# Activation, product and operand parts of an expert made for 64 or 128 slots by a branch on ScalarE and VectorE

## The chip, the cores and the metric

The kernel runs on one core of a Trainium2 chip. It uses TensorE for matrix products, VectorE and ScalarE for elementwise work, GpSimd a little, and SyncE for starting DMA transfers. Each engine works through an instruction queue of its own, and semaphores order them against each other. In the rows PE is TensorE (PEld its loading of the stationary operand), DVE is VectorE, ACT is ScalarE and SP is SyncE; a q behind a name means the engine's instruction queue. The metric is the device time of one execution in microseconds.

## The reference

A trunk of two layers on 256 tokens of width 1024, all in float32. Each layer has a mixer (gated linear attention and an SSD group) and a feed-forward part. The first layer's feed-forward part is dense, the second's is a mixture of 8 experts of which each token uses 2, and that is where the change is:

```python
def swiglu(t, w_gate, w_up, w_down):
    return (jax.nn.silu(t @ w_gate) * (t @ w_up)) @ w_down

top_v, top_i = lax.top_k(logits, TOP_K)
top_p = jax.nn.softmax(top_v, axis=-1)
gates = jnp.sum(jax.nn.one_hot(top_i, N_EXPERTS) * top_p[..., None], axis=1)
for e in range(N_EXPERTS):
    out = out + gates[:, e:e + 1] * swiglu(t, w_gate[e], w_up[e], w_down[e])
```

`w_gate[e]` and `w_up[e]` are 1024 x 3584, `w_down[e]` is 3584 x 1024.

## The kernel before

For each expert the kernel gathers the expert's tokens into slots (128 of them; a second pass behind the loop serves experts with more than 128 tokens, and is skipped here). The products are made from operands split in two parts, a rounded one and the rest, so that a product is a sum of three terms.

**Weights.** Every weight item is 1 MB in float32. SyncE's queue issues its transfer (`pump`, L154) into one of a few raw buffers as soon as one is free. ScalarE copies the item, rounded, into a slot (L182), VectorE subtracts the copy from the raw item into a second slot (L183), and from then on the raw buffer is free for the next transfer.

**An expert's loop.** `run_experts` walks through the items in the order of `moe_order`. The 3584 columns of an expert form 7 chunks of 512. A chunk has six items, G0 G1 (gate), U0 U1 (up) and D0 D1 (down) of the chunk before it. Behind certain items the dictionary `due` places the elementwise work: `copied` (ScalarE, L1229) brings a product out of PSUM; `gate` folds or transposes it on TensorE and applies Silu on ScalarE (L1253); `hidden` does the same for the up product and multiplies on VectorE (L1257); `parted` makes the two operand parts of the result, a copy on ScalarE (L1262) and a subtraction on VectorE (L1263). The tile `fsg` holds activation and product, `fth` the operand parts that the down product (`y`) uses.

**Narrow and wide.** `few[e]` is 1 where an expert has at most 64 tokens. `is_narrow` (L1578) loads it into a register of TensorE, and `modal` (L1177) makes a branch on it. In the narrow body of `mm_slots` the two operand parts of 64 slots lie side by side in one matmul's 128 columns (L1187), so that an item needs two matmuls per block and not three (L1189, L1190, and L1193 in both). The narrow body of `folded` adds the two halves of such a product with a matmul (L1238); the wide body transposes (L1240). Before the change only TensorE branches. ScalarE and VectorE do the same work for all 128 slots in either case.

**The next expert.** `at` hangs the next expert's preparation on items of this one: at chunk 3 the register and a slot map, at chunk 4 the gathering (TensorE) and splitting (`split_cols`: four ScalarE operations, a VectorE cast and a VectorE subtraction) of two halves of its operand, and between these two halves `slots_T`, for which VectorE makes a small tile `pm` (`pairs`, L1483) that TensorE transposes (L1508) and VectorE rounds off (L1511).

Of the kernel before, what the change touches and what calls it, by code (L numbers as in the profile page):

```python
# [50 lines left out]
def trunk(ctx: ExitStack, tc: tile.TileContext, a: dict, out: bass.AP):  # L51
# [1168 lines left out]
    def run_experts(mo, experts, operand, fold, at):  # L1220
# [11 lines left out]
        def folded(src, narrow, p):  # L1232

            def body(nar):
                for k in range(4):
                    ks = slice(k * P, (k + 1) * P)
                    if nar:
                        pe.matmul(p[:, ks], src[:, ks], fold, start=True, stop=True)  # L1238
                    else:
                        pe.transpose(p[:, ks], src[:, ks], ident)  # L1240

            modal(narrow, body)
            return p
# [7 lines left out]
        def gate(key):  # L1251
            sil[key] = mo.tile([P, FC], F, name=nm("fsg"), tag="fsg")
            act.activation(sil[key], folded(gs.pop(key), ops[key[0]][1], ps_t()), AF.Silu)  # L1253

        def hidden(key):
            p, s = folded(us.pop(key), ops[key[0]][1], ps_mm()), sil[key]
            dve.tensor_tensor(s, p, s, op=OP.mult)  # L1257

        def parted(key):
            t = th[key] = mo.tile([P, 4, P, 2], R, name=nm("fth"), tag="fth", bufs=2)  # L1260
            sv = sil.pop(key).rearrange("p (k t) -> p k t", k=4)
            act.activation(t[:, :, :, 0], sv, AF.Copy)  # L1262
            dve.tensor_tensor(t[:, :, :, 1], sv, t[:, :, :, 0].bitcast(F), op=OP.subtract)  # L1263

        for n, (kind, e, c, i) in enumerate(order):
# [3 lines left out]
            X, narrow = ops[e]  # L1269
# [71 lines left out]
    def moe(mo, ys, row, mT):  # L1341
# [235 lines left out]
        def is_narrow(e):  # L1577
            return pe.value_load(few[0:1, e:e + 1], min_val=0, max_val=1)  # L1578

        narrow = {0: is_narrow(0)}  # L1580
        pT = {0: slots_T(0, pm, narrow=narrow[0])}
        m = {"pm": pm, "y": {}, "acc": None}

        def free():
            return ps_y(1 - turn[0])

        def at(e, c, t, ys):
# [20 lines left out]
            if e < NE - 1:  # L1608
# [3 lines left out]
                if where == (4, 1):  # L1612
                    split_cols(*gathered(e + 1, 0), *gather(m["pm"], 0, free))
                if where == (4, 3):
                    pT[e + 1] = slots_T(e + 1, m["pm"], free, narrow[e + 1])
                if where == (4, 5):
                    split_cols(*gathered(e + 1, 1), *gather(m["pm"], 1, free))
# [12 lines left out]
        y = run_experts(mo, list(range(NE)), lambda e: (xg[e % 2], narrow[e]), fold, at)  # L1630
# [12 lines left out]
        with tc.If(over > 0):  # L1643
            xg.clear()
            for e in range(NE):
# [9 lines left out]
                y = run_experts(mo, [e], lambda e: (xg[e % 2], None), fold, lambda *_: None)  # L1655
# [129 lines left out]
```

## Time and the profile before

| | us |
|---|---|
| median of three runs | 1551.8 (1550.6 to 1554.3) |
| the profiled execution's own time | 1550.5 |
| its span | 1548.7 |
| TensorE busy in the span | 1410.1 (91%) |
| VectorE busy | 1310.8 (85%) |
| ScalarE busy | 1068.9 (69%) |
| expert phase in the span | 575 to 1531.6 |

The span is cut at the profile's first and last instruction. A busy share over the whole span mixes the first layer, the mixer and the expert phase, which have different limits. For the change only the expert phase matters, and inside it the experts with at most 64 tokens and those with more have to be looked at apart. The granted TensorE clock of the run is 0.967 of full speed.

### The profile page before, as it was taken

To read this page: it belongs to the slowest core of one execution; us is meant where nothing else is said; L and a number is where in the kernel's file an instruction comes from. 1 tells how busy PE (TensorE), PEld (TensorE's weight loads), DVE (VectorE), ACT (ScalarE), POOL (GpSimd) and SP (SyncE) were. 2 spreads that over 40 slices of the span, in tenths; PEclk is the share of its full clock that TensorE was granted. 3 is DMA by queue.
4 is the path that set the end of the run, shared out by engine and by line. 5 is a ranking of instruction groups with operands and counts; after the bars stand their busy time and mean duration, and the time that the engine had idled before them with its cause. 6 is when DMAs were issued, how large, how long until landed. Compare 5 with 4: busy or idle time off the path is not lost.

```text
span 1548.7 us, 20698 instructions
## 1 busy us (share of the span) xinstructions
PE 1410.1 (91%) x7578; PEld 1203.0 (78%) x7578; DVE 1310.8 (85%) x1171; ACT 1068.9 (69%) x1259; POOL 41.0 (3%) x68
## 2 busy tenths in 40 slices
PE   4998899999999877999999988989899999999986
PEld 3877699999888765878878767767778888878864
DVE  7898877777766758999879989989999888878996
ACT  3475554455557447987768779879898777768875
POOL 2001000000010100000000000000000000000001
PEclk8999999999999988999999989999999999999988
DMA  9975688888834454999979999999999999979992
GB/s 331 304 248 175 246 296 311 309 291 304 293 137 136 165 190 168 392 376 397 353 275 371 392 336 399 397 367 397 398 399 395 394 335 350 347 269 373 384 372 106
DMA packets 204603, 483.15 MB, mean 312 GB/s; under 512 B 13119, under 2 KB 15405, under 8 KB 204462
## 3 DMA queue, kind: packets, MB, share of 16 engines
q1 hardware_dynamic: 203890, 480.05, 85.1%
q8 instruction: 98, 1.61, 0.4%
q10 hardware_dynamic: 428, 0.63, 0.1%
q0 software_dynamic: 144, 0.52, 0.1%
q14 instruction: 43, 0.35, 0.1%
HBM read 480.12 MB, written 1.05 MB: 311 GB/s over the span
## 4 chain that ended last, share of the span: by engine, by line
PE 69%; DVE 15%; ACT 7%; issue 6%; DMA 2%; POOL 1%; DVEq 0%; ACTq 0%; SPq 0%; POOLq 0%
PE mm L1193 9%; DVE ws L183 6%; PE y L1193 6%; PE mm L1189 5%; PE mm L1190 5%; PE mm L1187 5%; PE mm L409 4%; PE mm L410 4%; PE mm L408 4%; PE y L1187 4%; PE y L408 3%; PE y L410 3%; PE y L409 3%; ACT ws L182 3%; PE y L1189 3%
## 5 line engine op out<-in xcount | busy, mean ns | idle before, releaser
L183 DVE TENSOR_TENSOR ws<-raw,ws 128x2048 fp32r<-128x2048 f32 x280 | 633.6, 2285 | 68.6 <-ACT ws L182 67.3
L182 ACT ACTIVATE ws<-raw 128x2048 fp32r<-128x2048 f32 x280 | 530.3, 1917 | 108.4 <-PE y L1190 34.4
L174 ACT ACTIVATE ws<-raw 128x1024 fp32r<-128x1024 f32 x138 | 145.9, 1061 | 133.7 <-PE mm L410 63.5
L175 DVE TENSOR_TENSOR ws<-raw,ws 128x1024 fp32r<-128x1024 f32 x138 | 166.7, 1220 | 56.0 <-ACT ws L174 55.6
L1193 PE MATMUL y<-ws,fth 128*128 128x512 f32 x448 | 128.4, 410 | 0.0
L1193 PE MATMUL mm<-ws,hTh 128*128 128x512 f32 x448 | 122.0, 394 | 1.1 <-DVE ws L183 1.1
L1193 PE MATMUL mm<-ws,hTl 128*128 128x512 f32 x448 | 121.8, 394 | 0.0
L347 DVE SCALAR_TENSOR_TENSOR ada<-raw,s_col,ada 128x1024 f32<-128x1024 f32 (+1 forms) x98 | 115.6, 1180 | 2.1
L183 DVE TENSOR_TENSOR ws<-xm,ws 128x2048 fp32r<-128x2048 f32 x46 | 105.2, 2287 | 9.3 <-ACT ws L182 8.9
L408 PE MATMUL mm<-hTh,ws 128*128 128x256 f32 x384 | 107.9, 281 | 0.0
L1193 PEld LDWEIGHTS y<-ws,fth 128*128 128x128 f32 x448 | 90.7, 202 | 20.7
L409 PE MATMUL mm<-hTh,ws 128*128 128x256 f32 x384 | 106.8, 278 | 0.0
L410 PE MATMUL mm<-hTl,ws 128*128 128x256 f32 x384 | 106.7, 278 | 0.0
L1193 PEld LDWEIGHTS mm<-ws,hTh 128*128 128x128 f32 x448 | 85.5, 191 | 20.2 <-DVE ws L183 1.6
L1193 PEld LDWEIGHTS mm<-ws,hTl 128*128 128x128 f32 x448 | 85.7, 191 | 18.1
L182 ACT ACTIVATE ws<-xm 128x2048 fp32r<-128x2048 f32 x46 | 88.3, 1920 | 12.2 <-PE mm L1190 6.6
L1187 PE MATMUL mm<-ws,hTh 128*128 128x512 f32 x336 | 94.9, 405 | 0.5 <-ACT ws L182 0.5
L1187 PE MATMUL y<-ws,fth 128*128 128x512 f32 x280 | 87.4, 438 | 6.8 <-DVE fth L1263 6.8
L1189 PE MATMUL mm<-ws,hTl 128*128 128x512 f32 x224 | 89.9, 401 | 0.0
L1190 PE MATMUL mm<-ws,hTl 128*128 128x512 f32 x224 | 88.5, 395 | 0.0
L1262 ACT ACTIVATE fth<-fsg 128x512 fp32r<-128x512 f32 x56 | 37.7, 673 | 64.6 <-DVE fsg L1257 64.5
L409 PEld LDWEIGHTS mm<-hTh,ws 128*128 128x128 f32 x384 | 72.3, 188 | 0.2
(381 smaller groups left out, 2816.4 us busy)
## 6 DMA issues: line engine op xcount, KB each, us to landing
raw<-in_moe_w_down SPq DMA_DIRECT2D x95, 1024.0 KB, 8.3
raw<-in_moe_w_up SPq DMA_DIRECT2D x94, 1024.0 KB, 8.1
raw<-in_moe_w_gate SPq DMA_DIRECT2D x92, 1024.0 KB, 7.3
raw<-in_ada_w SPq DMA_DIRECT2D x48, 1024.0 KB, 6.0
raw<-in_w_in SPq DMA_DIRECT2D x21, 1024.0 KB, 5.3
xm<-in_moe_w_up SPq DMA_DIRECT2D x16, 1024.0 KB, 5.9
xm<-in_moe_w_down SPq DMA_DIRECT2D x15, 1024.0 KB, 7.2
xm<-in_moe_w_gate SPq DMA_DIRECT2D x15, 1024.0 KB, 8.6
```

What stands on the lines that cost most here:

```text
L174: act.activation(h, src, AF.Copy)
L175: dve.tensor_tensor(lo, src, h.bitcast(F), op=OP.subtract)
L182: act.activation(h, r, AF.Copy)
L183: dve.tensor_tensor(lo, r, h.bitcast(F), op=OP.subtract)
L347: dve.scalar_tensor_tensor(acc, w, s_col[:, k:k + 1], acc, op0=OP.mult, op1=OP.add)
L408: pe.matmul(ps, xh, wh, start=start, stop=False)
L409: pe.matmul(ps, xl, wh, start=False, stop=False)
L410: pe.matmul(ps, xh, wl, start=False, stop=stop)
L1187: pe.matmul(ps, xs[:, 0:HALF].rearrange("p s two -> p (s two)"), wh, start=start, stop=False)
L1189: pe.matmul(ps, xs[:, :, 0], wh, start=start, stop=False)
L1190: pe.matmul(ps, xs[:, :, 1], wh, start=False, stop=False)
L1193: pe.matmul(ps, both if nar else xs[:, :, 0], wl, start=False, stop=stop)
```

## The change

`folded` loses its own branch. `gate`, `hidden` and `parted` each put their whole body into one branch: the folds on TensorE together with ScalarE's Silu; the folds with VectorE's product; ScalarE's copy with VectorE's subtraction. `blocks` cuts the tiles to the first 64 of each 128 columns in the narrow body, so a 128x512 operation becomes 128x4x64. `split_slots` does the same around `split_cols` for the next expert. `is_narrow` loads a second register, on TensorE, ScalarE and VectorE; TensorE's `mm_slots` and `slots_T` keep the first one.

```diff
--- before.py
+++ after.py
@@ -1229,18 +1229,18 @@
             act.activation(out, p, AF.Copy)
             return out
 
-        def folded(src, narrow, p):
-
-            def body(nar):
-                for k in range(4):
-                    ks = slice(k * P, (k + 1) * P)
-                    if nar:
-                        pe.matmul(p[:, ks], src[:, ks], fold, start=True, stop=True)
-                    else:
-                        pe.transpose(p[:, ks], src[:, ks], ident)
-
-            modal(narrow, body)
+        def folded(src, nar, p):
+
+            for k in range(4):
+                ks = slice(k * P, (k + 1) * P)
+                if nar:
+                    pe.matmul(p[:, ks], src[:, ks], fold, start=True, stop=True)
+                else:
+                    pe.transpose(p[:, ks], src[:, ks], ident)
             return p
+
+        def blocks(t, nar):
+            return t.rearrange("p (k t) -> p k t", k=4)[:, :, :HALF if nar else P]
 
         def put(n, f, *args):
             due.setdefault(n, []).append((f, args))
@@ -1249,24 +1249,41 @@
             (gs if kind == "G" else us)[key] = copied("gs" if kind == "G" else "us", ps.pop((kind,) + key))
 
         def gate(key):
-            sil[key] = mo.tile([P, FC], F, name=nm("fsg"), tag="fsg")
-            act.activation(sil[key], folded(gs.pop(key), ops[key[0]][1], ps_t()), AF.Silu)
+            src, p = gs.pop(key), ps_t()
+            s = sil[key] = mo.tile([P, FC], F, name=nm("fsg"), tag="fsg")
+
+            def body(nar):
+                folded(src, nar, p)
+                act.activation(blocks(s, nar), blocks(p, nar), AF.Silu)
+
+            modal(ops[key[0]][2], body)
 
         def hidden(key):
-            p, s = folded(us.pop(key), ops[key[0]][1], ps_mm()), sil[key]
-            dve.tensor_tensor(s, p, s, op=OP.mult)
+            src, p, s = us.pop(key), ps_mm(), sil[key]
+
+            def body(nar):
+                folded(src, nar, p)
+                sv = blocks(s, nar)
+                dve.tensor_tensor(sv, blocks(p, nar), sv, op=OP.mult)
+
+            modal(ops[key[0]][2], body)
 
         def parted(key):
             t = th[key] = mo.tile([P, 4, P, 2], R, name=nm("fth"), tag="fth", bufs=2)
-            sv = sil.pop(key).rearrange("p (k t) -> p k t", k=4)
-            act.activation(t[:, :, :, 0], sv, AF.Copy)
-            dve.tensor_tensor(t[:, :, :, 1], sv, t[:, :, :, 0].bitcast(F), op=OP.subtract)
+            s = sil.pop(key)
+
+            def body(nar):
+                sv, tv = blocks(s, nar), t[:, :, :HALF if nar else P]
+                act.activation(tv[:, :, :, 0], sv, AF.Copy)
+                dve.tensor_tensor(tv[:, :, :, 1], sv, tv[:, :, :, 0].bitcast(F), op=OP.subtract)
+
+            modal(ops[key[0]][2], body)
 
         for n, (kind, e, c, i) in enumerate(order):
             key = (e, c)
             if (kind, c, i) == ("G", 0, 0):
                 ops[e] = operand(e)
-            X, narrow = ops[e]
+            X, narrow, _ = ops[e]
             if kind in "GU" and not i:
                 ps[(kind,) + key] = ps_mm()
             if (kind, c, i) == ("D", 0, 0):
@@ -1575,14 +1592,25 @@
         fill()
 
         def is_narrow(e):
-            return pe.value_load(few[0:1, e:e + 1], min_val=0, max_val=1)
+            f = few[0:1, e:e + 1]
+            return pe.value_load(f, min_val=0, max_val=1), nc.values_load(
+                f, engines=[mybir.EngineType.PE, mybir.EngineType.Activation, mybir.EngineType.DVE], min_val=0, max_val=1)
 
         narrow = {0: is_narrow(0)}
-        pT = {0: slots_T(0, pm, narrow=narrow[0])}
+        pT = {0: slots_T(0, pm, narrow=narrow[0][0])}
         m = {"pm": pm, "y": {}, "acc": None}
 
         def free():
             return ps_y(1 - turn[0])
+
+        def split_slots(e, hf):
+            dst, (src, scale, shift) = gathered(e, hf), gather(m["pm"], hf, free)
+
+            def body(nar):
+                w = HALF if nar else P
+                split_cols(*[d[:, :, :w] for d in dst], src[:, :, :w], scale, shift)
+
+            modal(narrow[e][1], body)
 
         def at(e, c, t, ys):
             nonlocal acc, fnw
@@ -1610,11 +1638,11 @@
                     narrow[e + 1] = is_narrow(e + 1)
                     m["pm"] = slot_map(e + 1, 0)
                 if where == (4, 1):
-                    split_cols(*gathered(e + 1, 0), *gather(m["pm"], 0, free))
+                    split_slots(e + 1, 0)
                 if where == (4, 3):
-                    pT[e + 1] = slots_T(e + 1, m["pm"], free, narrow[e + 1])
+                    pT[e + 1] = slots_T(e + 1, m["pm"], free, narrow[e + 1][0])
                 if where == (4, 5):
-                    split_cols(*gathered(e + 1, 1), *gather(m["pm"], 1, free))
+                    split_slots(e + 1, 1)
             elif where in ((2, 5), (3, 3)):
                 t = c - 2
                 for hf in range(2):
@@ -1627,7 +1655,7 @@
                 m["y"][0] = y_split(ys[e], 0, g2)
 
         acc = fnw = None
-        y = run_experts(mo, list(range(NE)), lambda e: (xg[e % 2], narrow[e]), fold, at)
+        y = run_experts(mo, list(range(NE)), lambda e: (xg[e % 2],) + narrow[e], fold, at)
         extra.remove("xm")
         sq, write = finisher(fnw)
         y1 = mo.tile([P, 512], F, name=nm("ys"), tag="us")
@@ -1652,7 +1680,7 @@
                 assert state["next"] == first_item
                 pump()
                 fill()
-                y = run_experts(mo, [e], lambda e: (xg[e % 2], None), fold, lambda *_: None)
+                y = run_experts(mo, [e], lambda e: (xg[e % 2], None, None), fold, lambda *_: None)
                 for hf in range(2):
                     combine(e, pT, y_split(y, hf, g2), hf, False, acc)
             sq, write = finisher(load_fnw())
```

On VectorE, one chunk of expert 0 (`fsg` the activation and product, `fth` the operand parts, `ws` and `raw` weight slots and raw buffers). Before:

```order
L183 TENSOR_TENSOR ws_6328<-raw_794_6046,ws_6327 128x2048
L1257 TENSOR_TENSOR fsg_6267<-mm_6333,fsg_6267 128x512
L1177 UNCONDITIONAL_BRANCH
L183 TENSOR_TENSOR ws_6367<-raw_801_6096,ws_6366 128x2048
L1263 TENSOR_TENSOR fth_6372<-fsg_6267,fth_6372 128x512
L183 TENSOR_TENSOR ws_6397<-raw_804_6123,ws_6396 128x2048
```

After:

```order
L183 TENSOR_TENSOR ws_6394<-raw_795_6098,ws_6393 128x2048
L1177 COMPARE_AND_BRANCH
L1267 TENSOR_TENSOR fsg_6333<-mm_6399,fsg_6333 128x4x64
L1177 UNCONDITIONAL_BRANCH
L1267 TENSOR_TENSOR fsg_6333<-mm_6399,fsg_6333 128x512
L1177 UNCONDITIONAL_BRANCH x2
L183 TENSOR_TENSOR ws_6434<-raw_802_6149,ws_6433 128x2048
L1177 COMPARE_AND_BRANCH
L1278 TENSOR_TENSOR fth_6439<-fsg_6333,fth_6439 128x4x64
L1177 UNCONDITIONAL_BRANCH
L1278 TENSOR_TENSOR fth_6439<-fsg_6333,fth_6439 128x512
L1177 UNCONDITIONAL_BRANCH x4
```

The subtractions L183 stand where they stood. The product (L1257, now L1267) and the subtraction of the operand parts (L1263, now L1278) each stand twice, behind a compare: in four blocks of 64 and in 512 columns. An UNCONDITIONAL_BRANCH is a jump over the other body or to the next block.

On ScalarE, the same chunk, from the copy of the up product. Before:

```order
L1229 ACTIVATE us_6265<-mm_6212 128x512
L1253 ACTIVATE fsg_6267<-pt_6268 128x512
L1177 UNCONDITIONAL_BRANCH x2
L182 ACTIVATE ws_6300<-raw_791_6019 128x2048
L182 ACTIVATE ws_6327<-raw_794_6046 128x2048
L1177 UNCONDITIONAL_BRANCH x2
```

After:

```order
L1229 ACTIVATE us_6330<-mm_6277 128x512
L1177 COMPARE_AND_BRANCH
L1257 ACTIVATE fsg_6333<-pt_6332 128x4x64
L1177 UNCONDITIONAL_BRANCH
L1257 ACTIVATE fsg_6333<-pt_6332 128x512
L1177 UNCONDITIONAL_BRANCH x2
L182 ACTIVATE ws_6366<-raw_792_6071 128x2048
L1177 UNCONDITIONAL_BRANCH
L182 ACTIVATE ws_6393<-raw_795_6098 128x2048
L1177 COMPARE_AND_BRANCH
L1177 UNCONDITIONAL_BRANCH x3
```

The Silu (L1253, now L1257) stands twice behind a compare, and in front of the next subtraction's copy there is a second compare, that of the up product's branch, in which ScalarE has no work. The order of the working instructions is unchanged on each engine. In the whole program ScalarE and VectorE have 183 compares each where they had 1, TensorE 527 where it had 457, and the registers are loaded 9 times on ScalarE and VectorE (1 before) and 17 times on TensorE (9 before).

## Rows read from the trace of the kernel before

**Rows 1.** The page's part 1: busy us (share of the span) xinstructions, one line.
```profile
PE 1410.1 (91%) x7578; PEld 1203.0 (78%) x7578; DVE 1310.8 (85%) x1171; ACT 1068.9 (69%) x1259; POOL 41.0 (3%) x68
```

**Rows 2.** Experts 0 to 7 by stretch, expert 0 from 612: window, length, engines, PEclk, DMA share, GB/s.
```profile
575.00:689.30 114.30, 98.74 (x468) 80.66 (x467) 102.47 (x75) 95.08 (x80) 0.00 (x0) 0.91 0.83 304
689.30:822.40 133.10, 129.68 (x597) 108.32 (x596) 112.34 (x72) 98.58 (x81) 0.00 (x0) 0.99 0.95 347
822.40:935.40 113.00, 101.52 (x502) 84.33 (x500) 106.12 (x71) 93.06 (x80) 0.00 (x0) 0.95 0.99 368
935.40:1049.40 114.00, 100.39 (x492) 82.84 (x492) 108.72 (x72) 94.67 (x81) 0.00 (x0) 0.96 1.02 387
1049.40:1158.00 108.60, 98.62 (x493) 81.49 (x492) 108.38 (x72) 94.43 (x81) 0.00 (x0) 0.98 1.04 398
1158.00:1285.60 127.60, 127.60 (x598) 107.23 (x596) 113.75 (x73) 100.20 (x82) 0.00 (x0) 1.00 1.01 375
1285.60:1420.70 135.10, 131.68 (x605) 109.98 (x603) 111.56 (x72) 98.59 (x81) 0.76 (x1) 0.99 0.92 327
1420.70:1531.60 110.90, 101.39 (x475) 83.07 (x474) 107.37 (x71) 88.33 (x71) 0.00 (x0) 0.95 0.89 334
612.00:689.30 77.30, 73.21 (x371) 60.68 (x369) 76.53 (x50) 68.69 (x60) 0.00 (x0) 0.98 1.01 374
```

**Rows 3.** The page's part 5, TensorE's narrow matmul into y: busy, mean ns, idle before.
```profile
L1187 PE MATMUL y<-ws,fth 128*128 128x512 f32 x280 | 87.4, 438 | 6.8 <-DVE fth L1263 6.8
```

**Rows 4.** Waits of VectorE, ScalarE and SyncE's DMA queue, 822.4 to 1158: total us, times, longest.
```profile
DVE ws L183 <- ACT ws L182: 10.9, 7, 3.6
ACT fth L1262 <- DVE fsg L1257: 36.7, 19, 3.5
SPq L154 <- DVE ws L183: 268.3, 119, 6.9
```

**Rows 5.** Groups by page or tile (min/median/max ns, first to last start): VectorE, ScalarE durations.
```profile
L183 DVE TENSOR_TENSOR ws<-raw,ws 128x2048 fp32r<-128x2048 f32 x280 | 633.6, 2285 | 68.6 <-ACT ws L182 67.3
L1511 DVE TENSOR_SCALAR pTs<-y x7: 415/424/425, 658.3 to 1375.8; 128x256 fp32r<-128x256 f32 x7
L1257 DVE TENSOR_TENSOR fsg<-mm,fsg x56: 674/682/686, 604.6 to 1527.4; 128x512 f32<-128x512 f32 x56
L1253 ACT ACTIVATE fsg<-pt x56: 582/596/635, 595.4 to 1525.4; 128x512 f32<-128x512 f32 x56
L1262 ACT ACTIVATE fth<-fsg x56: 653/676/692, 605.3 to 1528.1; 128x512 fp32r<-128x512 f32 x56
```

**Rows 6.** Branches and register loads by line: count, min/median/max ns, first to last start.
```profile
L1177 PEldq COMPARE_BRANCH  x741: 63/176/396, 564.0 to 1530.0; - x186
L1643 DVEq COMPARE_BRANCH  x1: 72/72/72, 1539.7 to 1539.7; - x1
L1643 DVEq EVENT_SEMAPHORE  x1: 21/21/21, 1542.6 to 1542.6; - x1
L1643 PEldq COMPARE_BRANCH  x1: 3665/3665/3665, 1535.6 to 1535.6; - x1
L1642 DVEq TENSOR_LOAD <-cmi x1: 545/545/545, 1539.1 to 1539.1; - x1
```

**Rows 7.** VectorE's timeline in a chunk of expert 4: start us, us, instruction.
```profile
1102.45 2.28 DVE L183 TENSOR_TENSOR ws<-raw,ws 128x2048 fp32r<-128x2048 f32 x1
1104.65 0.68 DVE L1263 TENSOR_TENSOR fth<-fsg,fth 128x512 fp32r<-128x512 f32 x1
```

**Rows 8.** TensorE's wait for pm (total, longest; then by timeline), and two stretches around such places.
```profile
PE y L1508 <- DVE pm L1483: 13.6, 2, 6.8
899.25 0.73 PE L1508 MATMUL y<-ident,pm 128*128 128x128 f32 x2 [6.82 <-DVE pm L1483]
900.00:920.00 20.00, 20.00 (x93) 16.79 (x94) 14.38 (x11) 14.82 (x15) 0.00 (x0) 0.87 0.82 290
1015.00:1035.00 20.00, 20.00 (x100) 16.89 (x100) 15.28 (x11) 15.78 (x15) 0.00 (x0) 0.93 0.96 350
```

## The prediction

> **What bounds the kernel now.** I read the page's engine line first, then a table that cuts the expert phase into one stretch per expert, then the waits of the narrow stretch 822.4 to 1158, then single rows. Over the whole span TensorE leads with 1410.1 us, VectorE follows with 1310.8 and ScalarE has 1068.9 [rows 1], but this is an average over stages with different limits. The page's row of the narrow matmul into `y` has x280, that is 5 experts times 7 chunks times 8 [rows 3]: five of the eight experts have at most 64 tokens. The stretches say which. In experts 1, 5 and 6 TensorE is busy for 129.68 of 133.10, 127.60 of 127.60 and 131.68 of 135.10 us, and moves more instructions (597 to 605): these are the wide ones, and TensorE sets their time. Experts 0, 2, 3, 4 and 7 have only 468 to 502 matmuls and some 100 us of TensorE in 108 to 114, with VectorE above it: 106.12, 108.72, 108.38 and 107.37 in experts 2, 3, 4 and 7, and in expert 0, once its start is over, 76.53 of 77.30 [rows 2]. So in the narrow experts VectorE is the engine without a gap.
>
> It is not alone there. In expert 4 the DMA engines move 398 GB/s at a share of 1.04, and no stretch of this table shows more; experts 2 and 3 have 368 and 387. Experts 0 (from 612 us) and 7 have 374 and 334, so there the transfers have a reserve [rows 2]. The two are tied together: the queue that issues the weight transfers waits 119 times for a VectorE subtraction (L183), 268.3 us in all, since a raw buffer is free only when VectorE has read it. VectorE itself waits little for ScalarE, 10.9 us in 335, while ScalarE waits 36.7 us for the product L1257, so ScalarE has room [rows 4].
>
> **The change, part by part.** *VectorE's narrow product and operand part* (L1257, L1263): each of the 35 narrow chunks runs them on 256 elements per partition where it ran 512. No row of exactly this form exists, so I take the slope of VectorE's own rows: 2285 ns for 2048 elements and 682 for 512 give 1603/1536 = 1.04 ns per element, 0.267 us for 256 elements. A check is the 128x256 row of L1511: 424 ns, where 682 less 267 is 415 [rows 5]. Two such instructions give 0.53 us per chunk. From below, the saving is bounded at nothing if four blocks of 64 with gaps cost as much as 512 straight elements; from above at the whole 0.68 each. I take the slope, because the 424 ns row is so near.
>
> *ScalarE's narrow Silu and copy* (L1253, L1262): 596 and 676 ns at 512 elements [rows 5]. The cover is that ScalarE is busy for 94.43 of 108.60 us [rows 2] and waits for VectorE, not the other way round. At VectorE's slope it would save some 0.27 us each; I count nothing on the path. If ScalarE became the late one, this saving would help too.
>
> *The two operand halves of the next expert* shrink in the same way, 512 to 256 elements in a cast and a subtraction, 0.53 us on VectorE per half. Four experts gain it, but those of experts 2 and 7 are made inside wide experts, where TensorE hides it. The other two add 1.1 us each to VectorE's lead inside experts 2 and 3; I count it as reserve, since what I count there is limited otherwise (below).
>
> *TensorE's folds* keep their instructions and order. It passes 70 more branches (the operand parts and halves, which hold nothing for it). In the trace 741 such branches took 63 to 396 ns, median 176 [rows 6], and the queue reaches them while earlier matmuls run. I count nothing. If that cover were gone in the wide experts, 27 extra branches (21 chunks and 6 halves) at 0.176 would be 4.8 us.
>
> *Branches on ScalarE and VectorE* are new. Each chunk brings three to either engine (gate, product and part; one of the three is empty for each), each a compare and, on the narrow side, a jump over the other half. Nothing in the trace shows such branches on these engines inside the loop. The nearest rows are TensorE's, 176 ns for a compare and 63 for a jump, and VectorE's own compare after the loop, 72 ns [rows 6]. What hides them: VectorE's instructions of a narrow chunk stand back to back. L183 starts at 1102.45 and takes 2.28, L1263 starts at 1104.65 [rows 7], so its queue dispatches ahead of the one that is running. A branch behind a 2.28 us subtraction has that long to be decided. Behind the branches stand the next subtractions, and for these wait TensorE and the transfer queue. Bounds: nothing at one end, 3 x (0.176 + 0.063) = 0.72 us per chunk at the other. I take nothing, because two of the three branches stand behind a full subtraction; both ends are in the range.
>
> [...]
>
> *The second register* is loaded once per expert, on TensorE, ScalarE and VectorE. VectorE's load after the loop took 545 ns [rows 6]. At the head of the phase nothing is queued that could hide it, and I let one of the other seven be seen: 2 x 0.545 = **+1.1 us**.
>
> *Where the gain goes.* Expert 0 from 612 us: VectorE has no gap and the transfers a reserve, five chunks x 0.53 = **-2.7**. Expert 7: seven x 0.53 = **-3.7**. Wide experts: 0. Experts 2 to 4 form one run, and at 398 GB/s the transfers are full. What they can still gain is the time in which they slacken. At 899 us TensorE waits 6.8 us for VectorE's small `pm` operation, the longest wait of that stretch; around it the rate is 290 GB/s in 20 us, and around the same place in expert 3 it is 350 [rows 8]. Against 398 this is (398 - 290)/398 x 20 = 5.4 us and (398 - 350)/398 x 20 = 2.4 us of lost transfers. A VectorE that is ahead by then comes to `pm` earlier. It has gained 4 x 0.53 = 2.1 us by the first stall and 11 x 0.53 = 5.8 by the second, so I count 2.1 and the whole 2.4: **-4.5**. Expert 4 already runs at 398: 0.
>
> Sum: -2.7 - 3.7 - 4.5 + 1.1 = **-9.8 us**. The profiled run took 1550.5 us, of which 1548.7 are the span, so it would take 1540.7. The median shown is 1551.8, 1.3 above it; the same difference gives **1542.0 us**.
>
> **Rivals.** *Transfers are the only limit of experts 2 to 4.* Then their 4.5 us don't come: -5.3, 1546.5 us. For it: 398 GB/s, share 1.04. Against: the dips to 290 and 350, which have their cause on VectorE.
>
> *VectorE is the only limit in every narrow expert*, and the rate can rise above 398. Then 33 chunks x 0.53 = 17.5, less 1.1: 16.4, or 1535.4 us. Against it: no stretch goes above 398.
>
> *Jumps are exposed.* If on each of three branches a jump's 63 ns stay on VectorE's path, 33 x 0.19 = 6.2 us come back: -3.6 or 1548.2; with the first rival, +0.9 or 1552.7. What a measurement of this kernel can tell from no change is about 0.2%, 3.1 us, so this lies around "the same".
>
> *Branches are exposed in full, and it gets slower.* The place is VectorE's queue in a narrow chunk, the price 0.72 us against 0.53 saved: 33 x 0.19 = +6.2, 1558.0 us. It decides from 0.53/3 = 0.18 us per branch. For it: VectorE has no gap that could take them. Against it: the back-to-back starts, which show a queue running ahead [rows 7].
>
> [...] After the loop VectorE's compare at 1539.7 us is followed by its next instruction at 1542.6, 2.9 us later, and TensorE's far jump at the same line took 3665 ns [rows 6]. The narrow side takes a jump at each of 105 branches (35 chunks x 3). Were one in ten to cost 2.9, 10 x 2.9 = 29 us would stand against 9.8: +19, 1571 us. Some 3.4 such jumps eat the whole gain. Against it: those in the loop go over one instruction, the one at the end over a whole second pass, and none of TensorE's 741 passed 0.396. [...]
>
> **How the numbers follow.** Forecast 1542.0: 0.45. Transfers alone, 1546.5: 0.15. VectorE alone, 1535.4: 0.10. Jumps exposed, 1548.2 to 1552.7: 0.17, about a third of it still faster by over 0.2%. Exposed in full, 1558: 0.08. Fetches, 1571: 0.05. Faster by over 0.2% (under 1548.7): 0.45 + 0.15 + 0.10 + 0.05 = 0.75; within it 0.12; slower 0.13. The range leaves out the last two cases and ends with the others' outer times: 1535 to 1553.
>
> **What would show it.** Narrow products and parts on VectorE near 415 ns, with the wide ones still at 682. Expert 7 shorter by some 3.7 us, expert 0 by 2.7, experts 2 to 4 together by some 4.5 with the dips shallower, and experts 1, 5 and 6 unchanged. ScalarE's waits for the product should shrink. VectorE's gaps between a subtraction and the product or part behind it, now none, should stay under 0.1 us; gaps of 0.2 or more at every branch, or of 3 at a few, are the rivals. I would be wrong if four blocks of 64 cost as much as 512 elements, if a compare makes the engine run empty first, or if the transfers lose their reserve in experts 0 and 7 too.

## The result, and the profile after

The changed kernel takes 1540.5 us (median of five runs, 1536.1 to 1542.3), the kernel before, over five runs, 1553.7: a ratio of 0.9915 with a 95% interval of 0.990 to 0.993, 13.2 us less. The forecast was 1542.0 and -9.8 us.

The line of busy times of the page, after:

```profile
PE 1414.4 (92%) x7578; PEld 1208.0 (78%) x7578; DVE 1289.3 (84%) x1171; ACT 1056.3 (69%) x1259; POOL 41.0 (3%) x68
```

Against [rows 1] VectorE has lost 21.5 us and ScalarE 12.6; TensorE has gained 4.3. The span of this execution is 1540.4 us, only 8.3 below the one of before, since its expert phase starts later: TensorE's first weight product of expert 0 comes at 580.3 us in place of 575.0. VectorE's work is late by 5.2 us already at 566 us, ahead of the first expert and of every branch. The experts are therefore compared by their own lengths. The stretches of experts 0 to 7, from the first weight product of one to that of the next (window, its length, busy us of PE, PEld, DVE, ACT, POOL with counts, granted clock, DMA share, GB/s):

```profile
580.30:692.10 111.80, 99.11 (x467) 81.52 (x467) 99.37 (x75) 92.46 (x80) 0.00 (x0) 0.91 0.84 310
692.10:825.30 133.20, 129.66 (x595) 108.27 (x595) 110.75 (x72) 97.75 (x81) 0.00 (x0) 0.99 0.95 347
825.30:934.30 109.00, 100.36 (x502) 83.93 (x500) 102.16 (x71) 90.21 (x80) 0.00 (x0) 0.97 1.01 381
934.30:1044.10 109.80, 99.72 (x491) 82.56 (x491) 103.97 (x72) 91.74 (x81) 0.00 (x0) 0.97 1.04 398
1044.10:1153.30 109.20, 99.80 (x492) 81.35 (x491) 105.66 (x72) 93.75 (x81) 0.00 (x0) 0.98 1.04 398
1153.30:1280.90 127.60, 127.60 (x598) 107.24 (x596) 113.20 (x73) 100.49 (x82) 0.00 (x0) 1.00 1.01 377
1280.90:1416.10 135.20, 131.67 (x605) 110.02 (x603) 110.43 (x72) 98.14 (x81) 0.76 (x1) 0.99 0.92 328
1416.10:1523.00 106.90, 100.12 (x476) 82.72 (x474) 103.45 (x71) 85.36 (x71) 0.00 (x0) 0.97 0.91 345
```

Beside [rows 2]: expert 0 takes 111.8 us in place of 114.3, expert 2 takes 109.0 (113.0), expert 3 109.8 (114.0), expert 4 109.2 (108.6), and expert 7, to its last weight product, 108.3 (112.4). The wide experts 1, 5 and 6 take 133.2, 127.6 and 135.2 (133.1, 127.6, 135.1). All the gain lies in narrow experts, and expert 4 has none. There the DMA engines move 398 GB/s as before, and now in expert 3 too, and VectorE is no longer without a gap: it is busy for 105.66 of 109.20 us, where it was for 108.38 of 108.60.

Durations by tile (count, min/median/max ns, first and last start, forms); 35 of 56 executions are narrow:

```profile
L1267 DVE TENSOR_TENSOR fsg<-mm,fsg x56: 408/417/684, 609.7 to 1519.4; 128x256 f32<-128x256 f32 x35, 128x512 f32<-128x512 f32 x21
L1257 ACT ACTIVATE fsg<-pt x56: 369/397/595, 600.7 to 1517.5; 128x256 f32<-128x256 f32 x35, 128x512 f32<-128x512 f32 x21
L1278 DVE TENSOR_TENSOR fth<-fsg,fth x56: 410/419/690, 612.3 to 1520.4; 128x256 fp32r<-128x256 f32 x35, 128x512 fp32r<-128x512 f32 x21
L1277 ACT ACTIVATE fth<-fsg x56: 419/444/687, 610.2 to 1519.9; 128x256 fp32r<-128x256 f32 x35, 128x512 fp32r<-128x512 f32 x21
```

The narrow product and operand part take 417 and 419 ns on VectorE, where the slope had given 415. A tile view of the whole phase mixes both bodies, so the minimum and the median are of the narrow form and the maximum of the wide one.

The branches, and the loads of the second register, by line (count, min/median/max ns, first and last start):

```profile
L1177 PEldq COMPARE_BRANCH  x854: 63/176/421, 569.4 to 1521.4; - x171
L1177 ACTq COMPARE_BRANCH  x295: 34/38/50, 597.0 to 1519.9; - x148
L1177 DVEq COMPARE_BRANCH  x295: 43/47/69, 599.0 to 1520.4; - x148
L1596 ACTq TENSOR_LOAD <-few x8: 277/278/482, 572.5 to 1341.8; - x8
L1596 DVEq TENSOR_LOAD <-few x8: 299/313/556, 576.7 to 1342.8; - x8
```

In the median a branch on ScalarE takes 38 ns and on VectorE 47, against 176 on TensorE; each row holds compares and jumps together. VectorE's timeline in the chunk of expert 4 that answers to [rows 7] (start us, us, instruction) shows what they cost:

```profile
1095.39 0.41 DVE L1267 TENSOR_TENSOR fsg<-mm,fsg 128x256 f32<-128x256 f32 x1
1095.73 2.28 DVE L183 TENSOR_TENSOR ws<-raw,ws 128x2048 fp32r<-128x2048 f32 x1
1097.93 0.41 DVE L1278 TENSOR_TENSOR fth<-fsg,fth 128x256 fp32r<-128x256 f32 x1
1098.26 2.28 DVE L183 TENSOR_TENSOR ws<-xm,ws 128x2048 fp32r<-128x2048 f32 x1
```

The subtraction behind the product starts 0.34 us after it, the product taking 0.41, and the operand part starts where the subtraction ends. Nothing lies between them, though a compare stands ahead of each narrow instruction and a jump behind it.

### The profile page after: what moved, and what is told of

Read it like the earlier page. It is cut to its first block, busy times and chain, and to the rows that moved or that the text cites. A ratio compares the mean times of both kernels' runs of the same rounds, so it can differ in the third digit from the quotient of the medians.

```text
span 1540.4 us, 21495 instructions
## 1 busy us (share of the span) xinstructions
PE 1414.4 (92%) x7578; PEld 1208.0 (78%) x7578; DVE 1289.3 (84%) x1171; ACT 1056.3 (69%) x1259; POOL 41.0 (3%) x68
## 5 line engine op out<-in xcount | busy, mean ns | idle before, releaser
L183 DVE TENSOR_TENSOR ws<-raw,ws 128x2048 fp32r<-128x2048 f32 x280 | 634.0, 2285 | 74.2 <-ACT ws L182 73.1
L183 DVE TENSOR_TENSOR ws<-xm,ws 128x2048 fp32r<-128x2048 f32 x46 | 105.2, 2286 | 12.0 <-ACT ws L182 11.8
L1193 PEld LDWEIGHTS mm<-ws,hTh 128*128 128x128 f32 x448 | 85.8, 192 | 20.4 <-DVE ws L183 1.6
L1187 PEld LDWEIGHTS mm<-ws,hTh 128*128 128x128 f32 x336 | 62.2, 192 | 13.1 <-ACT ws L182 0.7
```

Of the source, the lines that this page charges most:

```text
L183: dve.tensor_tensor(lo, r, h.bitcast(F), op=OP.subtract)
L1187: pe.matmul(ps, xs[:, 0:HALF].rearrange("p s two -> p (s two)"), wh, start=start, stop=False)
L1193: pe.matmul(ps, both if nar else xs[:, :, 0], wl, start=False, stop=stop)
```

## The experiments

Every run was compared with the kernel before on the same chip. Besides the times I use the length of the **expert phase** in the profiled execution, from TensorE's first weight product to its last, since it leaves out the part in front, which starts the phase anywhere from 574.9 to 580.8 us. From the traces (us; TensorE's stalls that are spoken of below lie in experts 1, 2, 3 and 6; all numbers behind the ratio are of one execution):

| kernel | median us | ratio (95%) | phase | expert 0 | 2 | 3 | 4 | 7 |
|---|---|---|---|---|---|---|---|---|
| before | 1552.5 to 1554.2 | | 958.1 | 114.3 | 113.0 | 114.1 | 108.6 | 112.4 |
| changed | 1540.5 | 0.9915 (0.990 to 0.993) | 944.2 | 111.8 | 108.9 | 109.9 | 109.2 | 108.3 |
| changed again | 1539.7 | 0.9911 (0.9896 to 0.9926) | 943.5 | 109.9 | 109.0 | 111.9 | 107.7 | 108.3 |
| VectorE alone narrow | 1541.6 | 0.9921 (0.9905 to 0.9938) | 948.4 | 110.9 | 109.9 | 112.2 | 108.5 | 109.9 |
| halves whole | 1540.2 | 0.9920 (0.9903 to 0.9937) | 943.8 | 111.6 | 109.0 | 111.6 | 107.4 | 108.4 |
| branches doubled | 1540.4 | 0.9909 (0.9891 to 0.9926) | 944.4 | 111.6 | 108.9 | 112.2 | 108.0 | 108.3 |
| branches only | 1552.9 | 0.9996 (0.9985 to 1.0007) | 958.1 | 114.1 | 112.9 | 113.9 | 108.6 | 112.5 |
| ScalarE alone narrow | 1551.6 | 0.9987 (0.9978 to 0.9996) | 957.0 | 113.8 | 112.3 | 113.7 | 108.3 | 112.1 |
| light, before | 1553.4 | 1.0005 (0.9995 to 1.0015) | 958.3 | 114.3 | 112.7 | 113.9 | 108.6 | 112.5 |
| light, changed | 1537.1 | 0.9888 (0.9867 to 0.9909) | 943.0 | 111.4 | 108.8 | 111.4 | 106.4 | 108.4 |
| early pm, before | 1534.0 | 0.9879 (0.9862 to 0.9896) | 938.1 | 114.3 | 108.0 | 107.0 | 111.9 | 112.5 |
| early pm, changed | 1527.5 | 0.9819 (0.9798 to 0.984) | 930.0 | 111.9 | 102.7 | 111.3 | 110.7 | 108.4 |
| the same again | 1526.6 | 0.9826 (0.9813 to 0.984) | 927.7 | 109.9 | 102.7 | 110.2 | 112.0 | 108.4 |
| early pm, changed, light | 1513.7 | 0.9739 (0.9724 to 0.9754) | 916.1 | 109.9 | 102.7 | 104.2 | 106.4 | 108.4 |

### The changed kernel again

No edit.

> The changed kernel once more, beside the next three on one chip. Every theory expects a ratio to the kernel before of 0.990 to 0.993; it is the base for the others.

Ratio 0.9911, phase 943.5 us against 944.2: the result stands. Experts 0, 3 and 4 each differ by 1.5 to 2 us between the two executions, so a difference of that size in one expert of one profile says nothing.

### Branches without narrower operations

```diff
-            return t.rearrange("p (k t) -> p k t", k=4)[:, :, :HALF if nar else P]
+            return t.rearrange("p (k t) -> p k t", k=4)
-                sv, tv = blocks(s, nar), t[:, :, :HALF if nar else P]
+                sv, tv = blocks(s, nar), t
-                w = HALF if nar else P
+                w = P
```

> The same branches and registers, but both bodies work over 128 slots: the change without its narrower operations. Theory (branches and loads cost nothing that shows): ratio to before 0.999 to 1.002, -1 to +3 us. Rival (branches cost, and the narrower operations gain more than measured): by as much above before, 35 x 3 x 0.094 = +10 us if compare and jump are seen on VectorE each time, ratio 1.006.

Ratio 0.9996, and the phase has the same 958.1 us as before. The product keeps its old duration in all 56 executions, and VectorE passes as many branches as in the changed kernel (by tile, and by line):

```profile
L1267 DVE TENSOR_TENSOR fsg<-mm,fsg x56: 675/684/690, 608.7 to 1531.5; 128x512 f32<-128x512 f32 x56
L1177 DVEq COMPARE_BRANCH  x295: 43/47/69, 597.8 to 1533.0; - x148
```

Branches and registers by themselves cost nothing that can be measured, and the whole gain comes from the narrower operations. The theory held.

### Twice the branches

```diff
             modal(ops[key[0]][2], body)
+            modal(ops[key[0]][2], lambda nar: None)
```

The line is added in `gate`, `hidden` and `parted`.

> Behind each of a chunk's three branches stands a second one with nothing in it, on TensorE, ScalarE and VectorE: six branches per chunk in place of three. Theory (branches are hidden behind the operation that is running): within 1 us of the changed kernel. Rival (each compare and jump is seen on VectorE, at 0.047 us for either by the changed kernel's rows): 35 x 3 x 0.094 = +9.9 us, ratio near 0.998, and VectorE shows gaps of 0.1 us and more at every branch.

The branches by line (count, min/median/max ns, first and last start):

```profile
L1177 PEldq COMPARE_BRANCH  x1022: 63/176/406, 569.5 to 1521.2; - x171
L1177 ACTq COMPARE_BRANCH  x463: 34/38/50, 596.6 to 1519.9; - x155
L1177 DVEq COMPARE_BRANCH  x463: 43/47/63, 598.5 to 1520.4; - x155
```

VectorE and ScalarE pass 463 branch instructions in place of 295, 168 more each, at the same price, and the phase takes 944.4 us. An added branch has nothing in it, so these are compares alone, without jumps. At 47 ns the 168 would have been 7.9 us on VectorE, 4.9 of them (105) in the narrow experts, where VectorE sets the time; the phases of the two executions of the changed kernel are 944.2 and 943.5. The compares are hidden behind the operation that is running, as the back-to-back starts had suggested; the rival falls.

### VectorE alone narrow

```diff
-                act.activation(blocks(s, nar), blocks(p, nar), AF.Silu)
+                act.activation(blocks(s, False), blocks(p, False), AF.Silu)
-                act.activation(tv[:, :, :, 0], sv, AF.Copy)
+                act.activation(t[:, :, :, 0], blocks(s, False), AF.Copy)
-                w = HALF if nar else P
+                w = P
```

> Branches stay on both engines, but only VectorE's product and operand part are narrow; ScalarE's Silu and copy run over 512 columns in either body, and the next expert's operand halves over 128 slots. Theory (VectorE's 0.53 us per narrow chunk is all that counts, ScalarE has room): at most 2 us above the changed kernel, for the two halves made inside experts 2 and 3, and nothing for Silu and copy. Rival (ScalarE's 0.2 us per operation counts too, since VectorE's product follows the Silu and its subtraction the copy): 33 chunks x 0.4 = up to 13 us above, ratio to before near 1.0.

1541.6 us, ratio 0.9921. The tile view shows the Silu back at 593 ns and the product at 422:

```profile
L1267 DVE TENSOR_TENSOR fsg<-mm,fsg x56: 417/422/687, 606.5 to 1520.1; 128x256 f32<-128x256 f32 x35, 128x512 f32<-128x512 f32 x21
L1257 ACT ACTIVATE fsg<-pt x56: 582/593/634, 597.3 to 1518.2; 128x512 f32<-128x512 f32 x56
```

Most of the gain is there with VectorE alone: 9.7 us of the phase, where the changed kernel gains 14. The phase is 4 to 5 us longer than that of the changed kernel, 1.6 of them in expert 7; the medians differ by 1.9 us, with overlapping intervals. The rival's 13 us are excluded, but the theory's "nothing for Silu and copy" does not hold in the phase, as the next run shows.

### The next expert's halves whole

```diff
-                    split_slots(e + 1, 0)
+                    split_cols(*gathered(e + 1, 0), *gather(m["pm"], 0, free))
-                    split_slots(e + 1, 1)
+                    split_cols(*gathered(e + 1, 1), *gather(m["pm"], 1, free))
```

> The next expert's operand halves are made for 128 slots without a branch, all else as changed. Theory: 0 to 2 us above the changed kernel, since only two of the four experts concerned are prepared inside a VectorE-bound stretch, 2 x 0.53 us each. Rival (the branch around them costs what it saves, four ScalarE operations standing behind it): no difference or 1 us below.

1540.2 us and a phase of 943.8: no difference that can be measured. The narrower halves bring nothing. Since the run above has whole halves too, what it lacks against this one is ScalarE's Silu and copy alone: 4.6 us of the phase (948.4 to 943.8), 1.5 us by the medians.

### ScalarE alone narrow

VectorE's operations in the narrow body work on 512 elements again, each block of 64 slots taken twice:

```diff
-                sv = blocks(s, nar)
-                dve.tensor_tensor(sv, blocks(p, nar), sv, op=OP.mult)
+                if nar:
+                    dve.tensor_tensor(twice(src)[0], twice(p)[0], twice(s)[1], op=OP.mult)
+                else:
+                    dve.tensor_tensor(s, p, s, op=OP.mult)
...
+        def twice(t):
+            v = t.rearrange("p (k a t) -> p k a t", k=4, a=2)
+            return v, v[:, :, 0:1].to_broadcast([P, 4, 2, HALF])
```

The subtraction in `parted` is edited in the same way, and the halves are whole.

> Branches as changed, ScalarE's Silu and copy narrow, VectorE's product and operand part at 512 elements in the narrow body too (each 64-slot block twice), the halves for 128 slots. Theory (VectorE's time is what counts): nothing gained, ratio to before 0.998 to 1.001, expert phase (TensorE's first to last weight product) within 2 us of the 958.1 us of before, where the changed kernel has 944.2 and 943.5. Rival (ScalarE's narrower work has a share of its own): up to 33 x 0.4 = 13 us less; the vector-only run left room for some 2 to 4.

By tile, the Silu is narrow and the narrow body's product is at its old 682 ns:

```profile
L1261 ACT ACTIVATE fsg<-pt x56: 363/392/607, 597.0 to 1525.5; 128x256 f32<-128x256 f32 x35, 128x512 f32<-128x512 f32 x21
L1272 DVE TENSOR_TENSOR us<-mm,fsg x35: 674/682/687, 606.1 to 1527.6; 128x512 f32<-128x512 f32 x35
```

Ratio 0.9987, with an interval that ends at 0.9996: some 2 us, 1.1 in the phase, which is inside the theory's range. But four kernels with the same branches and whole halves now stand beside each other. Their phases are 958.1 us with neither engine narrow, 957.0 with ScalarE, 948.4 with VectorE and 943.8 with both. So ScalarE's narrower work is worth 1.1 us by itself and 4.6 once VectorE is narrow. VectorE does wait for ScalarE at times [rows 4], which I had not turned into a number.

### Lighter transfers, before and changed

Of each down item of experts 2 to 4 only the first half is transferred; the other half of the buffer keeps what an earlier item left.

```diff
-            r = big(taken[i], shape)
+            if i in light:
+                r = last[taken[i]]
+                if r.shape[1] == 4:
+                    r = r.rearrange("p (a b) n -> p a (b n)", a=2)
+            else:
+                r = last[taken[i]] = big(taken[i], shape)
...
-            sp.dma_start(r, view)
+            if i in light:
+                sp.dma_start(r[:, :1], view[:, :1])
+            else:
+                sp.dma_start(r, view)
```

> The kernel before, but of the down items of experts 2 to 4 only the first half is transferred (the other half of the buffer keeps what it held, so the result differs): a sixth less traffic in these experts, so that 398 GB/s can't limit them. Theory: experts 2 to 4 were at VectorE's limit with the transfers just below theirs; lighter transfers give the 5 to 8 us that were lost around the two stalls, experts 2 to 4 take some 328 to 331 us in place of 335.6. Rival (transfers were the limit): over 10 us less.

> The changed kernel with the same lighter transfers. Theory: VectorE is now alone the limit of experts 2 to 4, and they are shorter than with the lighter kernel before by 21 chunks x 0.53 = 11 us plus 1 to 2 for the halves: some 316 to 319 us, 9 us less than the 328.0 of the changed kernel. Rival (in the changed kernel the transfers don't limit these experts): 0 to 3 us less than 328.

Experts 2 to 4 of the lighter kernel before (columns as above):

```profile
822.90:935.60 112.70, 102.53 (x502) 85.34 (x499) 106.09 (x71) 93.15 (x80) 0.00 (x0) 0.95 0.88 310
935.60:1049.40 113.80, 100.17 (x491) 82.82 (x491) 108.64 (x72) 94.61 (x81) 0.00 (x0) 0.96 0.91 324
1049.40:1158.10 108.70, 98.69 (x494) 81.64 (x492) 108.47 (x72) 94.50 (x81) 0.00 (x0) 0.98 0.95 340
```

They move 310 to 340 GB/s in place of 368 to 398, and the three take 335.2 us in place of 335.6. Both expectations miss: transfers limited nothing in the kernel before, and the time around the stalls was not lost by them. ScalarE's waits in experts 2 to 4 of the kernel before agree: besides the wait for the product [rows 4] there are only these (total us, times, longest), none for a transfer:

```profile
ACT ws L182 <- PE y L1187: 11.6, 5, 4.9
ACT sct L464 <- PE y L1490: 3.4, 2, 1.7
ACT ws L182 <- PE mm L1187: 1.5, 3, 0.8
ACT ws L182 <- PE y L1190: 0.9, 1, 0.9
```

Experts 2 to 4 of the lighter changed kernel:

```profile
821.00:929.80 108.80, 100.16 (x500) 83.72 (x499) 102.09 (x71) 90.16 (x80) 0.00 (x0) 0.97 0.90 322
929.80:1041.20 111.40, 101.39 (x493) 83.77 (x492) 104.16 (x72) 91.21 (x81) 0.00 (x0) 0.95 0.92 331
1041.20:1147.60 106.40, 98.76 (x492) 81.43 (x491) 106.10 (x73) 92.79 (x82) 0.00 (x0) 0.98 0.98 352
```

326.6 us, 1.4 to 2.0 less than with full traffic (328.0 and 328.6) and far from the 316 to 319 of the theory. Here the rival held: the ceiling takes 1 to 2 us of the changed kernel, little more than what two executions differ by. It shows in expert 4 above all, where ScalarE now waits for transfers. The largest of ScalarE's waits for VectorE and for transfers in experts 2 to 4 of the changed kernel (total us, times, longest):

```profile
ACT fth L1277 <- DVE fsg L1267: 21.2, 16, 2.8
ACT ws L182 <- DMA raw<-in_moe_w_down: 8.2, 15, 0.8
```

Its wait for the product is down from 36.7 to 21.2 us. Transfers are waited for 12.5 us in all, the 8.2 us of the row above and smaller ones, 9.5 of them in expert 4; with the lighter transfers no such wait is left.

### The pm operations placed earlier

What was left unexplained were the two stalls in experts 2 and 3. In the changed kernel TensorE's wait for `pm` in experts 2 to 4 (total us, times, longest) and the 20 us behind each of the two places, cut as in [rows 8], are:

```profile
PE y L1525 <- DVE pm L1500: 11.3, 2, 6.4
900.00:920.00 20.00, 20.00 (x96) 16.76 (x97) 14.14 (x12) 15.00 (x15) 0.00 (x0) 0.89 0.93 341
1011.00:1031.00 20.00, 20.00 (x103) 17.09 (x103) 15.13 (x11) 16.12 (x16) 0.00 (x0) 0.94 1.04 398
```

Against [rows 8] the wait is 11.3 us in place of 13.6, so it has stayed, while the dips behind it are shallower: 341 and 398 GB/s, where it was 290 and 350. I moved the two `pm` operations ahead, from behind U1 of chunk 4 to behind U1 of chunk 3; with six items in a chunk these are six items, not the four that the expectation names.

```diff
                     m["pm"] = slot_map(e + 1, 0)
+                if where == (3, 3):
+                    pairs(e + 1)
...
-            if narrow is not None:
+            if narrow is not None and not early:
                 pairs(e)
```

> The changed kernel, with the two small pm operations of the narrow map placed four items earlier (behind item U1 of chunk 3 in place of U1 of chunk 4). Theory: TensorE's wait for pm (6.4 us, twice in experts 2 to 4) and VectorE's idle 3.5 us behind it go; where VectorE is the limit (experts 2 and 3) this gives up to 3.5 us each, but experts 2 to 4 together already move 398 GB/s in expert 3 and 4, so I expect 0 to 4 us, and 3 us in the wide experts 1 and 6, where TensorE is the limit and waits 3.3 us: 3 to 8 us below the changed kernel. Rival (the wait is replaced by the next one, that of the transposed map's copy or the first matmul behind it): within 1 us.

> The kernel before with the early pm operations alone. Theory (TensorE's wait for pm costs its own length and VectorE's idle time behind it, on whichever engine is the limit): the same 12 to 15 us that it gave on top of the changed kernel, ratio 0.990 to 0.992; with VectorE the limit in experts 2 to 4 and the transfers still below their ceiling it may be less, 8 us. Rival (the two overlap: a VectorE that is ahead is what made the early pm pay): under 5 us.

> The changed kernel with early pm once more, beside the early kernel before. Every theory expects a ratio to before of 0.981 to 0.985. The changed part alone is worth the distance to the early kernel before: 13 us if it adds up, less where the transfers at 398 GB/s take it (theory: 8 to 12 us).

It gives more than any theory expected: on top of the changed kernel 12 to 14 us by the medians and 13 to 17 by the phase, where I had said 3 to 8, and 19 to 20 us on the kernel before, where I had said 12 to 15. TensorE's wait for `pm` is gone from the loop. In the kernel before there were four such waits, one each in experts 1, 2, 3 and 6, of 20.2 us in all, and the phase is 20.0 us shorter without them; but the experts share this unevenly. The dip is gone with the wait: in the early kernel before, the 20 us behind the same transposes read

```profile
890.00:910.00 20.00, 19.89 (x107) 16.69 (x106) 19.78 (x15) 19.68 (x20) 0.00 (x0) 1.00 1.04 396
```

Around these waits the granted clock fell as well. Two stretches around the stall of expert 2 in the kernel before (same columns):

```profile
895.00:905.00 10.00, 5.75 (x14) 4.46 (x15) 5.98 (x6) 4.09 (x4) 0.00 (x0) 0.50 1.04 396
905.00:915.00 10.00, 10.00 (x57) 8.60 (x57) 7.85 (x7) 7.91 (x9) 0.00 (x0) 0.99 0.72 246
```

TensorE waits 6.8 us, and the granted clock over the 10 us around the wait's end is 0.50 of full speed; the next stretch is back at 0.99 and has no gap on TensorE. With early `pm`, the stretch and the row of the same transposes, which now come at 887.7 us:

```profile
883.00:893.00 10.00, 9.70 (x51) 7.68 (x51) 9.54 (x9) 9.06 (x12) 0.00 (x0) 1.00 1.04 398
887.71 0.38 PE L1525 MATMUL y<-ident,pm 128*128 128x128 f32 x2
```

The clock stays at 1.00, and the two transposes take 0.38 us where they took 0.73 [rows 8]. In the wide experts 1 and 6, where TensorE is the limit, the wait was 3.3 us by the trace of before, and each became some 5.7 us shorter (133.3 to 127.5 and 135.2 to 129.5). Behind the wait of expert 1, which ends at 776.9 us in the kernel before, the clock falls while TensorE is busy:

```profile
778.00:780.00 2.00, 2.00 (x8) 1.65 (x7) 0.00 (x0) 0.00 (x0) 0.00 (x0) 0.74 1.01 362
780.00:782.00 2.00, 2.00 (x6) 1.54 (x6) 0.00 (x0) 1.63 (x1) 0.00 (x0) 0.50 0.56 210
782.00:784.00 2.00, 2.00 (x10) 1.63 (x9) 1.69 (x1) 0.28 (x1) 0.00 (x0) 0.91 0.00 0
```

The three fall short of the full clock by 0.26, 0.50 and 0.09 of 2 us, 1.7 us together, so by an estimate from these rows the clock takes 1.7 of the 2.4 us by which this expert gains more than its wait. The matmuls into `y` at 779.3 and 779.7 us take 0.63 us each; in the early, changed kernel those behind the same transposes take 0.39 from the second on. In experts 2 to 4 it is the other way round: the kernel before loses waits of 13.6 us there and gains 8.8 (335.6 to 326.8), as expert 4 gets longer (108.6 to 111.9).

Change and early `pm` don't add up in full. In the phase the change is worth 14 us without early `pm` (958.1 to 944.2), and 8 to 10 with it (938.1 to 930.0 and 927.7; 6.6 and 7.4 by the medians). The next kernel says what takes the rest.

### Early pm with lighter transfers

The edits of the early and of the light kernel together.

> The changed kernel with early pm, and only the first half of each down item of experts 2 to 4 transferred (the result differs). Experts 3 and 4 took 222.0 us in the early kernel, 84 MB at 396 GB/s. Theory (there the transfers are now the limit): with a sixth less traffic they fall to VectorE's time, 2 x 104 to 106 us, so 10 to 14 us less than 222. Rival (VectorE or the order on TensorE is the limit there): within 3 us of 222.

Experts 3 and 4 of the early kernel (columns as above), and then of the early, light one:

```profile
922.10:1033.50 111.40, 100.75 (x494) 81.13 (x492) 106.27 (x72) 94.99 (x81) 0.00 (x0) 0.98 1.04 398
1033.50:1144.10 110.60, 99.89 (x491) 80.95 (x491) 105.37 (x71) 93.65 (x81) 0.00 (x0) 0.98 1.04 398
```

```profile
919.80:1024.00 104.20, 98.27 (x493) 81.69 (x492) 103.71 (x72) 90.89 (x81) 0.00 (x0) 0.98 0.99 354
1024.00:1130.40 106.40, 98.82 (x493) 81.32 (x492) 106.10 (x73) 92.71 (x82) 0.00 (x0) 0.98 0.98 353
```

With full traffic both move 398 GB/s at a share of 1.04 and take 222.0 us; with a sixth less, 210.6, and VectorE is busy for 103.71 of 104.20 and 106.10 of 106.40. So once the stalls are gone, transfers limit experts 3 and 4 in the early kernel and VectorE is right behind. This expectation held. Since the light kernels leave data out, the version to keep is the early, changed one: 1526.6 and 1527.5 us, ratios 0.9826 and 0.9819, below both kernels.

## Why the prediction was right, and where it was off

**What bounds.** VectorE in the narrow experts, TensorE in the wide ones: right. Wide experts moved by 0.1 us in the first execution, narrow ones carry the gain, and narrowing VectorE alone gives 9.7 of the 14.3 us of the phase that both engines give together. The second limit was put too early: in the kernel before, transfers at 398 GB/s in expert 4 were full but not late. A high rate and share showed that they kept up with VectorE, since the queue that issues the transfers waits for VectorE to free a buffer (119 times [rows 4]); they did not show who waited. ScalarE's waits would have shown it: in experts 2 to 4 none of them was for a transfer.

**VectorE's instructions**: 415 forecast, 417 and 419 measured. **Branches**: taken as nothing, and nothing they are, by the branches-only and the doubled kernel. The upper bound had rested on TensorE's row, its median of 176 and minimum of 63 ns read as compare and jump, though it holds both together; VectorE's own median is 47. The rival at 1571 us, fetches by the forecast's name, fell too, but not by the length of the branches, at most 69 ns on VectorE: the compare behind the loop has only 72 ns itself, and yet 2.9 us pass to the next instruction [rows 6]; that a fetch takes them no row shows. It fell by the phase, which with all of these jumps and no narrower operation is the 958.1 us of before.

**The second register**: 1.1 us forecast. The loads take 278 and 313 ns in the median, and as the branches-only kernel shows no loss they are hidden or lost in the noise.

**The sum by experts.** Expert 7: -3.7 forecast, -4.1 in both executions. That these are so near is in part luck: the term was VectorE's, and VectorE alone gave 2.5 us there (112.4 to 109.9), the rest coming with ScalarE, which was counted at nothing. Expert 0: -2.7 forecast, -2.5 and -4.4. Experts 2 to 4: -4.5 forecast, -7.6 and -7.0. This is the term that was mis-sized, and the step that failed is "What they can still gain is the time in which they slacken", with its 2.1 and 2.4 us around the two stalls. [rows 2] already had more room: at 398 GB/s experts 2 and 3, which moved 368 and 387, would have been 8.5 and 3.2 us shorter, 11.7 together, and the early, changed kernel uses nearly all of it (335.6 to 324.7 and 324.9 us). Nor were the transfers what held these experts: the lighter kernel before shows that the dips to 290 and 350 GB/s were no loss, since with less to move the three took the same time. The dips were a consequence of the stall and went with it. They did get shallower, as forecast, but a VectorE that was ahead did not come to `pm` much earlier: the wait is 11.3 us in place of 13.6. What came instead is VectorE's own saving, chunk by chunk, 21 x 0.53 = 11.1 us by the forecast's price, of which 8.6 us are seen with light transfers (335.2 to 326.6) and 7.0 to 7.6 with full ones. The ceiling thus takes 1 to 2. For the other 2.5 the lighter kernels show where they stay: VectorE is busy for 10.9 us less (323.2 to 312.4) and idle for 2.3 more, 1.7 of them in longer waits for ScalarE's copies (10.8 to 12.5). Why these grow I can only argue: behind each stall TensorE has no gap for some 20 us [rows 8], and what VectorE saves there is not on the path.

**ScalarE**: counted at nothing, worth 1.1 us of the phase by itself and 4.6 once VectorE is narrow. **The halves**: counted as reserve, and worth nothing by the run with whole halves.

So the forecast's direction and mechanism were right, with the size between its likeliest case (-9.8) and the rival in which VectorE is alone the limit (-16.4). The transfers had more room than was granted to them, but not where this rival sought it: it wanted a rate above 398 GB/s, and no expert of the changed kernel shows one. The room lay below 398, in experts 2 and 3.

## What to carry to other kernels

A transfer queue that ran at its highest rate was not yet the limit here, where the engine behind it frees the buffers: expert 4 of the kernel before moved 398 GB/s, and with a sixth less traffic experts 2 to 4 took 335.2 us in place of 335.6. So look for waits on transfers, or lighten the traffic and see. A branch over short instructions may be put on an elementwise engine if its queue runs ahead: at a median of 38 and 47 ns the branches cost nothing here (a phase of 958.1 us with and without them). So narrowing work by a value known at run time was worth mainly what the narrower instructions saved on the engine that sets the time, 9.7 of 14.3 us; the other engine's share came only together with it. A small operation late in one engine's queue stalled another: TensorE waited up to 6.8 us for VectorE's two `pm` operations of 0.34 us, and its granted clock was 0.50 around the end of that wait. Moving the two gave 19 to 20 us on the kernel before, more than the 13 to 14 of the whole change.

## What was unexpected of the hardware

In the median a branch is cheaper on ScalarE (38 ns) and VectorE (47 ns) than on TensorE's queue (176 ns), and doubling the compares cost nothing in time (a phase of 944.4 us, where the changed kernel has 944.2 and 943.5). A wait of TensorE of 6.8 us left the granted clock at 0.50 for the 10 us around its end, and behind a wait of 3.3 us the clock fell to 0.50 while TensorE was busy again. In experts 1 and 6, where TensorE is the limit, the stall was dearer than the wait that the profile lists: without their waits of 3.3 us they became some 5.7 us shorter, in expert 1 by the estimate above 1.7 us of it through the clock.
